# First modulation group taken straight as columns, and three products for one more feed-forward block, in a two-layer hybrid trunk on one core

## The chip, the core and the metric

The kernel runs on one core of a Trainium2 chip. A core has TensorE (PE: matrix products; its weight loads have a row of their own, PEld), VectorE (DVE), ScalarE (ACT), GpSimd (POOL) and SyncE (SP, which here only issues transfers). They work through queues of their own and wait for each other by semaphores. The metric is the device time of one execution in microseconds (us).

## The reference, cut to what matters

Two layers, each with a token mixer and a gated convolutional feed-forward. The mixer of layer 0 is a bidirectional mLSTM over 256 context and 256 latent tokens; that of layer 1 is latent attention, for which only the 256 latent tokens go on. Every sublayer's input is shifted and scaled by a modulation that is a product of a conditioning vector with a large matrix:

```python
def _modulation(cond, w, b):
    m = jax.nn.silu(cond) @ w + b
    return jnp.split(m[:, None, :], 6, axis=-1)
...
    hl = _modulate(x, ml[0], ml[1])         # x * (1 + scale) + shift
    hc = _modulate(xc, mc[0], mc[1])
...
def _conv_ffn(h, w_in, conv_w, conv_b, w_out):
    gate, up = jnp.split(h @ w_in, 2, axis=-1)
    return (jax.nn.silu(_dwconv(gate, conv_w, conv_b)) * up) @ w_out
```

There are two conditioning vectors (latent and context), the model width is 1024, and the matrix of one layer is 1024 x 6144. The first thing that the kernel needs is the shift and scale of layer 0's mixer, 2 x 1024 columns of that matrix.

## The kernel before, in words

**Precision.** Every fp32 operand is split into a high part (cast to fp32r by ACT, L388 or L323) and a low part (the difference, by DVE, L389 or L326). A product of two such operands is three matmuls, high-high, high-low, low-high (`mm3`, L383 to L385).

**Start.** `start_up` begins the mixer's up-projection while its inputs still arrive. The 1024 features are cut into four groups of 256 (`GROUPS`, 2 blocks of 128 each). `LOADS` lists the transfers in SP's order: `a` = the group's modulation weights (8 pieces into 4 tiles of 128 x 1024, L609), `r` = a weight tile of the up-projection, `x` = token tiles. `STEPS` lists by hand the order of work, and the order on PE, DVE and ACT is kept as written:

- `S g`: split the group's 4 modulation tiles (`ada_split`).
- `A g`: `ada_rows`, L474. The conditioning (128 x 4: two vectors, high and low) is the stationary operand, the weights stream through with 512 columns: 16 matmuls for 8 blocks of k and two parts, summed to a row block of 4 x 512. ACT copies it out of PSUM (L477).
- `T g`: `ada_T`, L484. Four transposes turn the rows into columns, 128 x 4 each.
- `M g`: `ada_cols` (L494, L495, DVE) adds the parts and the bias; `mod_tiles` scales and shifts the group's token tiles (L570, L572) and splits them into `hT`.
- `W m`: split up-projection weight tile m.
- `D n`: n products of a zero tile with itself into a PSUM tile that nobody reads ("idle", L659).
- two digits `m g`: the products of up tile m for group g.

The order of the steps of group 0 was S0, W0, A0, D3, T0, D6, M0.

**Last feed-forward.** `ffn_in` makes, for each of the 22 channel blocks p of 128, a gate tile (j = 0) and an up tile (j = 1) from 8 blocks of k. In layer 1 there are 256 tokens, and high and low parts of the input lie side by side (`both`). For p = 0 a tile takes three products of 256 columns a step of k. For p > 0 it takes two (L1320): the weights' high part with both parts of the input at once (512 columns, into the two halves of the PSUM tile), and the weights' low part with the high part (256 columns). Then ACT copies the right half out (L1323) and DVE adds it to the left (L1324), and the convolution (L668 to L675) and the gating (L1330) read that sum.

Of the kernel before, what the change touches and what calls it, by code (L numbers as in the profile page):

```python
# [47 lines left out]
GROUPS = ((0, 2), (2, 4), (4, 6), (6, 8))  # L48
LOADS = [(c[0], int(c[1])) for c in "a0 r0 r1 x0 r2 a1 r3 r4 x1 a2 x2 x3 a3".split()]
STEPS = [(c[0], int(c[1])) for c in (  # L50
    "S0 W0 A0 D3 T0 D6 M0 W1 W2 S1 00 01 W3 W4 A1 03 T1 M1 02 04 10 11 S2 A2 12 T2 M2 13 14 21 "
    "S3 20 A3 24 T3 22 23 M3 31 32 33 34 30").split()]

TAIL = {"mout": 4, "aout": 7, "fout1": 6}
# [300 lines left out]
class K:  # L355
# [97 lines left out]

    def ada_split(self, g):
        r = []
        for w in self.adaw.pop(g):
            hi, lo = [self.pool.tile([128, 1024], F32R, tag="u", name="adas", bufs=NU) for _ in range(2)]
            self.split(hi, lo, w)
            r.append((hi, lo))
        return r  # L460

    def ada_rows(self, g, parts):

        nc = self.nc
        f0, f1 = GROUPS[g]
        nf = f1 - f0
        n = 256 * nf
        pr = self.ps("adar")
        for i, (hi, lo) in enumerate(parts):
            for kk in range(1024 // n):  # L470
                k = i * (1024 // n) + kk
                c = slice(kk * n, (kk + 1) * n)
                for x in (hi, lo):
                    nc.tensor.matmul(pr[0:4, :n], self.condr[:, k, :], x[:, c], start=k == 0 and x is hi,  # L474
                                     stop=k == 7 and x is lo)
        r = self.s2("adarow")
        nc.scalar.copy(r[0:4, :n], pr[0:4, :n])  # L477
        return r
# [105 lines left out]
    def start_up(self):  # L584

        nc, st = self.nc, self.st
        self.hT = []
        self.xcd = self.dr.tile([16, 128, 512], F32, name="xcd")
        self.xmd = self.dr.tile([16, 128, 512], F32, name="xmd")
        self.t2d = {(n, p, j): self.dr.tile([128, 1024], F32, name="t2d")  # L590
                    for n, a, b in (("v", 2, 4), ("y", 1, 6)) for p in range(a) for j in range(b)}
        self.xA, self.x1, self.xc, self.xcr = {}, {}, [], []
        w, ps, raws = [], [], []
        src = self.a["ada_w"][0]
        self.adaw, self.xT = {}, []
        for op, g in LOADS:
            f0, f1 = GROUPS[g] if op != "r" else (0, 0)
            if op == "a":
                wd = 128 * (f1 - f0)
                nk = 512 // wd  # L600
                self.adaw[g] = []
                for k in range(8):
                    if k % nk == 0:
                        t = self.uf("adaw")
                        self.adaw[g].append(t)
                    ap = bass.AP(tensor=src.tensor, offset=src.offset + k * 128 * 6 * D + f0 * 128,
                                 ap=[[6 * D, 128], [D, 2], [1, wd]])
                    c = k % nk * 2 * wd
                    nc.sync.dma_start(t[:, c:c + 2 * wd].rearrange("p (a b) -> p a b", a=2), ap)  # L609
            elif op == "x":  # L610
                for i in range(f0, f1):
                    x = self.s2("xT")
                    nc.sync.dma_start(x, self.a["tokT"][i])
                    self.xT.append(x)
            else:
                n, _ = st.ids["up", g, 0]
                r = self.pool.tile([128, 1024], F32, tag="raw" if g < 3 else "ar", name="raw0",
                                   bufs=NRAW if g < 3 else 2)
                nc.sync.dma_start(r, st.ws[n])
                raws.append(r)  # L620

        def wsplit(m):
            if m < 3:
                t = self.pool.tile([128, 2, CW], F32R, tag="w", name="w", bufs=NB)
                h, l = t[:, 0], t[:, 1]
            elif m == 3:
                h, l = [self.pool.tile([128, CW], F32R, tag="acc", name="w0", bufs=2) for _ in range(2)]
            else:
                h, l = [self.pool.tile([128, CW], F32R, tag="u", name="w0", bufs=NU) for _ in range(2)]
            self.split(h, l, raws[m])  # L630
            w.append((h, l))
            ps.append(self.ps("up"))

        def part(g, ms):
            for m in ms:
                for k in range(*GROUPS[g]):
                    c = slice(k * 128, (k + 1) * 128)
                    self.mm3(ps[m], (w[m][0][:, c], w[m][1][:, c]), (self.hT[k][:, 0], self.hT[k][:, 1]),
                             k == 0, k == 7)

        e = mybir.EngineType
        idle = self.ps("idle")
        rows = {}
        with self.tc.manual_schedule(engines={e.PE, e.DVE, e.Activation}):
            for op, g in STEPS:
                if op == "S":
                    rows[g] = self.ada_split(g)
                elif op == "A":
                    rows[g] = self.ada_rows(g, rows[g])
                elif op == "T":  # L650
                    rows[g] = self.ada_T(g, rows[g])
                elif op == "M":
                    self.ada_cols(g, rows.pop(g))
                    self.mod_tiles(range(*GROUPS[g]))
                elif op == "W":
                    wsplit(g)
                elif op == "D":
                    for _ in range(g):
                        nc.tensor.matmul(idle, self.zero[:, 0:128], self.zero, start=True, stop=True)  # L659
                else:  # L660
                    part(int(op), [g])
        for m in range(NUP):
            self.up_evac(m, ps[m])
# [628 lines left out]
    def ffn_in(self, l, hT, n, nt, pre=(), both=None):  # L1292

        nc, st = self.nc, self.st
        cw, cb = self.smc("fcw%d" % l), self.smc("fcb%d" % l)
        key = "fin%d" % l
        acts = []
        pre = list(pre)
        for p in range(NF):
            pss = []  # L1300
            for j in range(2):
                if pre:
                    w, ps = pre.pop(0)
                    self.ffn_half(ps, w, hT, 1)
                    if not pre:
                        st.unhold()
                else:
                    w = st.use((key, p, j))
                    ps = self.ps("fin")
                    two = ps.rearrange("p (a t) -> p a t", a=2)  # L1310
                    for k in range(8):
                        c = slice(k * 128, (k + 1) * 128)
                        hi, lo = hT(k)
                        if both is None or p == 0:
                            self.mm3(ps[:, :n], (w[0][:, c], w[1][:, c]), (hi, lo), k == 0, k == 7)
                            continue

                        mms = [(two, w[0][:, c], both(k)), (ps[:, :n], w[1][:, c], hi)]
                        for i, (o, a, b) in enumerate(mms if k < 7 else mms[::-1]):
                            nc.tensor.matmul(o, a, b, start=k == 0 and i == 0, stop=k == 7 and i == 1)  # L1320
                    if both is not None and p > 0:
                        t = self.s2("fs")
                        nc.scalar.copy(t[:, n:2 * n], ps[:, n:2 * n])  # L1323
                        nc.vector.tensor_tensor(t[:, :n], ps[:, :n], t[:, n:2 * n], op=ALU.add)  # L1324
                        ps = t
                pss.append(ps)
                self.tick(nt, ADA_F if p else 0)
            tmp = self.s2("fg")
            self.conv(pss[0], [cw[:, j * NF + p:j * NF + p + 1] for j in range(3)], cb[:, p:p + 1], tmp, n)
            nc.vector.tensor_tensor(tmp[:, :n], tmp[:, :n], pss[1][:, :n], op=ALU.mult)  # L1330
            if l == 0:
                if p % 2:
                    self.act_sums(p // 2, acts.pop(), tmp)
                else:
                    acts.append(tmp)
                continue
            a = self.u("act")
            nc.scalar.copy(a[:, 0, :n], tmp[:, :n])
            nc.vector.tensor_sub(a[:, 1, :n], tmp[:, :n], a[:, 0, :n])
            acts.append(a)  # L1340
        return acts
# [642 lines left out]
```

## Time and profile before

| | |
|---|---|
| median of 3 runs | 1386.9 us (1386.04 to 1388.71) |
| the profiled execution | 1386.22 us |
| its span, first to last instruction | 1384.1 us |
| PE busy | 1354.0 us, 98% of the span |
| DVE busy | 1090.0 us, 79% |
| ACT busy | 713.1 us, 52% |
| mean granted clock of PE | 0.996 |

A row of the timeline reads: start in us, length in us, engine, line of the kernel, operation, output<-input, shapes, count, and in brackets the idle time before it and what ended it. "x4" rows are merged: the length goes from the first's start to the last's end. Matmuls are pipelined, so one's record is longer than the distance between two. A row of the groups reads: line, engine, operation, shapes, count, then busy us and mean ns of one, then idle time before them. A row of the stretches reads: from:to, length, then the busy time of PE, PEld, DVE, ACT and POOL, the granted clock of PE, the share of the DMA engines, GB/s.

### The profile page before, as it was taken

How to read it: one execution, taken by the hardware profiler on the slowest of the kernel's cores; microseconds unless marked ns; L12 is line 12 of the kernel's file. 1: busy time of each engine (PE TensorE's matmuls, PEld its weight loads, DVE VectorE, ACT ScalarE, POOL GpSimd, SP SyncE). 2: the span in 40 equal slices, each digit the busy share in tenths (PEclk: the TensorE clock that was granted, in tenths of full speed). 3: DMA queues.
4: the chain of work that ended last, by engine and by line, in shares of the span. 5: the costliest groups of instructions: out<-in, count | busy, mean ns of one | idle time of the engine just before them, and what ended most of it. 6: DMA issues, size and time to landing. Idle time of an engine off the chain costs nothing.

```text
span 1384.1 us, 18592 instructions
## 1 busy us (share of the span) xinstructions
PE 1354.0 (98%) x6567; PEld 1123.2 (81%) x6567; DVE 1090.0 (79%) x1768; ACT 713.1 (52%) x1221; POOL 121.6 (9%) x215
## 2 busy tenths in 40 slices
PE   7999999999999999999999999999999999999997
PEld 3788888888788888878898888888777888888886
DVE  6598857687688697779799878668898789788873
ACT  6585534435444555364643434334637567466660
POOL 0033000011011011120002000000001001000100
PEclk9999999999999999999999999999999999999999
DMA  9689847789666364766747877646987425256750
GB/s 338 227 293 316 290 156 247 239 286 302 214 200 204 105 232 132 250 193 228 241 147 239 300 230 234 212 145 229 312 231 226 137 99 202 109 185 185 252 202 31
DMA packets 97900, 297.58 MB, mean 215 GB/s; under 512 B 12136, under 2 KB 24808, under 8 KB 97808
## 3 DMA queue, kind: packets, MB, share of 16 engines
q1 hardware_dynamic: 68672, 218.52, 47.5%
q0 software_dynamic: 17472, 57.57, 13.3%
q10 hardware_dynamic: 11664, 20.32, 4.1%
q8 instruction: 51, 0.84, 0.2%
q14 instruction: 41, 0.34, 0.1%
HBM read 262.90 MB, written 33.46 MB: 214 GB/s over the span
## 4 chain that ended last, share of the span: by engine, by line
PE 91%; DVE 5%; ACT 2%; issue 1%; DMA 0%; SPq 0%; DVEq 0%; ACTq 0%
PE fin L1320 9%; PE fin L383 6%; PE fin L384 6%; PE fin L385 6%; PE tok L383 6%; PE tok L384 6%; PE tok L385 6%; PE y L384 5%; PE y L385 5%; PE y L383 5%; PE qk L383 4%; PE qk L385 4%; PE qk L384 4%; PE up L383 2%; PE up L385 2%; PE up L384 2%
## 5 line engine op out<-in xcount | busy, mean ns | idle before, releaser
L326 DVE TENSOR_TENSOR w<-raw,w 128x1024 fp32r<-128x1024 f32 (+3 forms) x290 | 348.1, 1203 | 141.3 <-ACT w L323 140.3
L323 ACT CAST w<-raw 128x1024 fp32r<-128x1024 f32 (+3 forms) x290 | 300.4, 1037 | 306.2 <-PE tok L385 88.6
L512 DVE SCALAR_TENSOR_TENSOR junk<-ar,bc 128x1024 f32<-128x1024 f32 x128 | 156.0, 1218 | 4.9 <-ACT bc L554 2.1
L384 PE MATMUL fin<-h,w 128*128 128x512 f32 (+1 forms) x376 | 141.2, 376 | 0.0
L385 PE MATMUL fin<-h,w 128*128 128x512 f32 (+1 forms) x376 | 140.9, 375 | 0.0
L383 PE MATMUL fin<-h,w 128*128 128x512 f32 (+1 forms) x376 | 140.8, 376 | 0.1
L1320 PE MATMUL fin<-h,w 128*128 128x256 f32 (+1 forms) x640 | 113.0, 339 | 0.0
L1320 PEld LDWEIGHTS fin<-h,w 128*128 128x128 f32 x640 | 98.2, 189 | 14.7
L383 PE MATMUL qk<-xc,w 128*128 128x512 f32 x256 | 100.7, 393 | 0.0
L385 PE MATMUL qk<-xc,w 128*128 128x512 f32 x256 | 99.9, 390 | 0.0
L384 PE MATMUL qk<-xc,w 128*128 128x512 f32 x256 | 99.8, 390 | 0.0
L384 PEld LDWEIGHTS fin<-h,w 128*128 128x128 f32 x376 | 70.8, 188 | 12.9 <-DVE h L1212 0.2
L385 PEld LDWEIGHTS fin<-h,w 128*128 128x128 f32 x376 | 70.8, 188 | 12.9
L383 PEld LDWEIGHTS fin<-h,w 128*128 128x128 f32 x376 | 70.5, 188 | 13.1 <-ACT h L1211 0.3
L383 PEld LDWEIGHTS qk<-xc,w 128*128 128x128 f32 x256 | 48.1, 188 | 10.0 <-issue 0.4
L385 PEld LDWEIGHTS qk<-xc,w 128*128 128x128 f32 x256 | 48.1, 188 | 9.9
L384 PEld LDWEIGHTS qk<-xc,w 128*128 128x128 f32 x256 | 48.1, 188 | 9.7
L383 PE MATMUL up<-hT,w 128*128 128x512 f32 x128 | 50.5, 394 | 0.5 <-ACT hT L388 0.5
L384 PE MATMUL up<-hT,w 128*128 128x512 f32 x128 | 50.1, 392 | 0.5 <-DVE hT L389 0.5
L385 PE MATMUL up<-hT,w 128*128 128x512 f32 x128 | 50.1, 391 | 0.3 <-DVE w L389 0.3
L383 PE MATMUL tok<-w,hT 128*128 128x512 f32 x128 | 49.8, 389 | 0.0
L384 PE MATMUL tok<-w,hT 128*128 128x512 f32 x128 | 49.8, 389 | 0.0
(463 smaller groups left out, 3151.2 us busy)
## 6 DMA issues: line engine op xcount, KB each, us to landing
raw<-in_ws SPq DMA_DIRECT2D x287, 512.0 KB, 4.3
ar<-in_adaT SPq DMA_DIRECT2D x80, 512.0 KB, 4.6
adaw<-in_ada_w SPq DMA_DIRECT2D x32, 256.0 KB, 6.7
t2d<-raw ACTq DMA_DIRECT2D x13, 512.0 KB, 4.9
raw<-t2d SPq DMA_DIRECT2D x13, 512.0 KB, 6.3
raw<-in_ws POOLq DMA_DIRECT2D x13, 512.0 KB, 8.0
zr<-fd ACTq DMA_DIRECT2D x33, 128.0 KB, 3.9
xmd<-xr POOLq DMA_DIRECT2D x16, 256.0 KB, 5.0
```

What stands on the lines that cost most here:

```text
L323: k.nc.scalar.copy(h[:, :cols], src)
L326: k.nc.vector.tensor_sub(l[:, :cols], src, h[:, :cols])
L383: mm(out, w[0], x[0], start=start, stop=False)
L384: mm(out, w[0], x[1], start=False, stop=False)
L385: mm(out, w[1], x[0], start=False, stop=stop)
L512: nc.vector.scalar_tensor_tensor(o, w, 1.0, self.bc[j], op0=ALU.mult, op1=ALU.mult, accum_out=col[:, k, j:j + 1])
L1320: nc.tensor.matmul(o, a, b, start=k == 0 and i == 0, stop=k == 7 and i == 1)
```

## The change

Group 0's modulation gets a step of its own, `C`, in place of `A` and `T`. `ada_direct` makes the weights the stationary operand, 128 columns at a time, and the conditioning the moving one, 4 columns wide: the result comes as columns, in the layout that the transposes gave. For each of 8 blocks of k, for the high and the low part, and for 4 column blocks there is one matmul, 64 in all, into one PSUM tile. After each of the first three weight tiles two idle products follow. The last weight tile of group 0 is split in two halves of 512 columns. The order becomes S0, D2, C0, W0, D5, M0. In `ffn_in` the three-product form is used for p < 2 instead of p = 0.

```diff
 STEPS = [(c[0], int(c[1])) for c in (
-    "S0 W0 A0 D3 T0 D6 M0 W1 W2 S1 00 01 W3 W4 A1 03 T1 M1 02 04 10 11 S2 A2 12 T2 M2 13 14 21 "
+    "S0 D2 C0 W0 D5 M0 W1 W2 S1 00 01 W3 W4 A1 03 T1 M1 02 04 10 11 S2 A2 12 T2 M2 13 14 21 "
     "S3 20 A3 24 T3 22 23 M3 31 32 33 34 30").split()]
...
     def ada_split(self, g):
         r = []
-        for w in self.adaw.pop(g):
+        ws = self.adaw.pop(g)
+        for w in ws:
             hi, lo = [self.pool.tile([128, 1024], F32R, tag="u", name="adas", bufs=NU) for _ in range(2)]
-            self.split(hi, lo, w)
+            n = 512 if g == 0 and w is ws[-1] else 1024
+            for i in range(0, 1024, n):
+                self.split(hi[:, i:i + n], lo[:, i:i + n], w[:, i:i + n])
             r.append((hi, lo))
         return r
+
+    def ada_direct(self, g, parts, idle):
+
+        f0, f1 = GROUPS[g]
+        n = 2 * (f1 - f0)
+        pt = self.ps("adat")
+        for i, (hi, lo) in enumerate(parts):
+            for kk in range(8 // n):
+                k = i * (8 // n) + kk
+                for x in (hi, lo):
+                    for j in range(n):
+                        c = (kk * n + j) * 128
+                        self.nc.tensor.matmul(pt[:, 4 * j:4 * j + 4], x[:, c:c + 128], self.condr[:, k, :],
+                                              start=k == j == 0 and x is hi, stop=k == 7 and j == n - 1 and x is lo)
+            for _ in range(2 if i + 1 < len(parts) else 0):
+                self.nc.tensor.matmul(idle, self.zero[:, 0:128], self.zero, start=True, stop=True)
+        return pt
...
+                elif op == "C":
+                    rows[g] = self.ada_direct(g, rows[g], idle)
...
-                        if both is None or p == 0:
+                        if both is None or p < 2:
                             self.mm3(ps[:, :n], (w[0][:, c], w[1][:, c]), (hi, lo), k == 0, k == 7)
                             continue
...
-                    if both is not None and p > 0:
+                    if both is not None and p > 1:
                         t = self.s2("fs")
                         nc.scalar.copy(t[:, n:2 * n], ps[:, n:2 * n])
```

## The prediction

> **What bounds the kernel now.** I read the page's first, second and fourth parts, to see which engine sets the end.
>
> ```profile
> span 1384.1 us, 18592 instructions
> PE 1354.0 (98%) x6567; PEld 1123.2 (81%) x6567; DVE 1090.0 (79%) x1768; ACT 713.1 (52%) x1221; POOL 121.6 (9%) x215
> PE 91%; DVE 5%; ACT 2%; issue 1%; DMA 0%; SPq 0%; DVEq 0%; ACTq 0%
> ```
>
> TensorE (PE) is busy 98% of the span and owns 91% of the chain that ended last. So an edit is worth something in two places only: where PE's own work gets longer or shorter, and where PE stands idle. The busy time by stretches (PE is the first column after the length) says where it stands idle.
>
> ```profile
> 26.80:590.00 563.20, 563.17 (x2541) 459.06 (x2539) 426.72 (x675) 280.32 (x480) 64.92 (x114) 1.00 0.70 232
> 590.00:1185.00 595.00, 585.04 (x2910) 493.47 (x2908) 498.46 (x826) 305.92 (x534) 45.71 (x81) 1.00 0.65 213
> 1196.00:1376.00 180.00, 180.00 (x1009) 156.49 (x1008) 134.83 (x212) 102.74 (x170) 9.82 (x16) 1.00 0.51 168
> ```
>
> From 26.8 on PE hardly stops; what happens before 26.8 shifts everything behind it one for one. The first edit lies in those 27 us, the second at 1196, where PE has no gap at all. The chain in order of time shows the start:
>
> ```profile
> 4.72 5.90 DMA adaw<-in_ada_w
> ...
> 10.64 1.06 ACT adas L388
> ...
> 11.73 1.24 DVE adas L389
> ...
> 13.01 0.86 PE adar L474 x3
> 13.87 0.69 PE idle L659 x3
> 14.56 0.40 PE adat L484 x4
> ...
> 14.98 0.18 DVE adt L494
> ```
>
> The chain runs through the last weight tile's load, its cast, its subtraction, the last row products, the copy of the row (hidden here behind "idle"), the transposes, and the add. All of the start hangs on the moment at which VectorE (DVE) begins L494: 14.98. Behind L494 on DVE and behind L572, which waits for it, on ScalarE (ACT) stand, in order, the first token tiles and the splits W1, W2, S1, W3, W4:
>
> ```profile
> 19.37 2.36 DVE L389 TENSOR_TENSOR w<-raw,w 128x1024 fp32r<-128x1024 f32 x2 [0.26 <-ACT w L388]
> 21.65 4.62 DVE L389 TENSOR_TENSOR adas<-adaw,adas 128x1024 fp32r<-128x1024 f32 x4
> 26.19 2.35 DVE L389 TENSOR_TENSOR w<-raw,w 128x1024 fp32r<-128x1024 f32 x2
> ```
>
> DVE works there without a gap for 9 us and none of these rows waits for a DMA, so a later L494 is not caught up. **The first edit's worth is the new start of L494 minus 14.98.**
>
> **The change part by part.** Before, group 0 takes 16 products with 4 weight columns and 512 moving columns, a copy and four transposes. After, it takes 64 products (8 k, high and low half, 4 column blocks), each loading 128 weight columns for 4 moving ones. When the operands come does not change, for the casts hang on the DMA and the subtractions on the casts:
>
> ```profile
> 0.95 0.48 DVE L436 MEMSET zero<- 128x512 f32 x1
> ...
> 6.79 0.59 PE L474 MATMUL adar<-adas,condr 128*4 128x512 f32 x1 [6.79 <-ACT adas L388]
> 8.05 1.87 PE L474 MATMUL adar<-adas,condr 128*4 128x512 f32 x4 [0.67 <-DVE adas L389]
> 10.12 2.56 PE L474 MATMUL adar<-adas,condr 128*4 128x512 f32 x8 [0.20 <-DVE adas L389]
> 11.73 1.23 DVE L389 TENSOR_TENSOR adas<-adaw,adas 128x1024 fp32r<-128x1024 f32 x1 [0.19 <-ACT adas L388]
> 13.01 0.86 PE L474 MATMUL adar<-adas,condr 128*4 128x512 f32 x3 [0.33 <-DVE adas L389]
> 16.69 0.50 PE L383 MATMUL up<-hT,w 128*128 128x512 f32 x1 [0.16 <-ACT hT L388]
> ```
>
> The high half of tile 0 is there at 6.79, its low half at 8.05; those of tiles 1 and 3 at 10.12 and 12.96 (11.73 + 1.23), and that of tile 2 between. The rows also give the clock. At 8.05 four products need 1.87: (1.87 - 0.59)/3 = 0.43 a product. At 13.01 three need 0.86: (0.86 - 0.39)/2 = 0.23, with 0.39 for a single one at full speed (L384 below). So PE runs at half speed at first; the eight products from 10.12 on take 2.56, which is two slow distances and five fast ones with the 0.39 and a short wait, so the clock rises at about 10.95.
>
> *Price of one weight load and product.* The trace has no 128-column fp32r load before a 4-column product, so I bound it. Durations of loads (mean ns is the last number before the second bar):
>
> ```profile
> L474 PEld LDWEIGHTS adar<-adas,condr 128*4 128x4 f32 x64 | 5.0, 87 | 20.8 <-ACT adas L388 7.1 <-DVE adas L389 6.8 <-issue 1.1
> L857 PEld LDWEIGHTS gates<-xc,w 128*32 128x32 f32 x32 | 3.5, 109 | 3.8
> L383 PEld LDWEIGHTS qk<-xc,w 128*128 128x128 f32 x256 | 48.1, 188 | 10.0 <-issue 0.4
> L1754 PEld LDWEIGHTS PT<-ident,P 128*128 128x128 f32 x64 | 7.2, 140 | 0.1
> 14.53 0.32 PEld L484 LDWEIGHTS adat<-ident,adarow 4*128 4x128 f32 x4 [0.40 <-ACT adarow L477]
> 14.53 0.41 PE L484 MATMUL adat<-ident,adarow 4*128 4x4 f32 x4
> L384 PE MATMUL qk<-xc,w 128*128 128x512 f32 x256 | 99.8, 390 | 0.0
> L484 PE MATMUL adat<-ident,adarow 4*128 4x4 f32 x4 | 0.4, 203 | 0.0
> 1190.85 0.41 PE L383 MATMUL fin<-h,wu 128*128 128x256 f32 x1
> 1191.06 0.41 PE L384 MATMUL fin<-h,wu 128*128 128x256 f32 x1
> 1194.04 0.28 PE L385 MATMUL fin<-h,wu 128*128 128x256 f32 x1
> ...
> 1196.56 0.28 PE L385 MATMUL fin<-h,wu 128*128 128x256 f32 x1
> ```
>
> A product's fp32r load lasts 87 ns at 4 columns, 109 at 32 and 188 at 128: (188 - 109)/96 = 0.82 ns a column, so 128 columns hold the load path about 105 ns. Upper row: 256-column products with 128-column loads start every (1196.56 - 1194.04)/21 = 0.12; load and stream both fit in that. Lower row: the transposes, also 128 columns loaded for 4 moving ones, pass at (0.41 - 0.20)/3 = 0.07 (by their loads 0.06); but their kind of load lasts 140 at 128 columns (L1754), not 188. **I take 0.12**, as the new loads are of the 188 kind, and keep 0.06 as the other end. At half speed the 256-column products start every 1191.06 - 1190.85 = 0.21, so 0.21 there, and 0.12 for the cheap end.
>
> *The sum of the first edit.* From 8.05, twelve pairs of tile 0 at 0.213: 2.56, to 10.61. Two idle products across the rise, 0.43 + 0.23, to 11.27. Tile 1: 16 x 0.12 = 1.92, to 13.19; two idle 0.46, to 13.65; tile 2 to 15.57; idle to 16.03; tile 3 to 17.95. No tile waits for its low half any more: PE itself is the bound. The last product starts 0.12 before that, ends 0.20 later (18.03), and L494 starts at 18.06 instead of 14.98: **+3.1 us**. The copy and the transposes that go are in this difference already.
>
> The other pieces lie under this. D2 can run from about 1.5 us, once the zero tile is written (L436), and PE has nothing until 6.79; without that cover it would cost 0.86. D5 (5 x 0.23 = 1.15) ends before the first "up" product, which needs both adds, a modulation and a cast after L494: 16.69 - 14.98 = 1.7; D6 was hidden in the same way. Halving the last tile gives ACT and DVE one more instruction each and lets DVE start earlier; PE reaches tile 3 only at 16.03, so it neither gains nor costs; were PE faster, the halves would save about four pairs. W0's cast and subtraction come before M0 on both engines as before, and are done long before 18. SP's queue is untouched, POOL has nothing here.
>
> The added wait is L494's on PE, 3 us longer. Queued behind it are M0 and the five splits above; PE's "up" products wait for those, with nothing else to do.
>
> Bounds: at the full clock from 8.05 on, the same sum ends L494's wait at 16.75 (+1.8). The rise comes at the end of a stretch whose phase nothing here fixes; each us that it comes later adds about 0.44. At 0.107 a pair instead of 0.12, the 48 fast pairs save 0.6.
>
> *The second edit.* For the second channel block of the last feed-forward, 16 steps of k (2 tiles of 8) go from two products (512 and 256 columns) to three of 256.
>
> ```profile
> 1196.68 5.78 PE L1320 MATMUL fin<-h,wu 128*128 128x512 f32 x32
> 1202.30 9.90 PE L1320 MATMUL fin<-h,w 128*128 128x512 f32 x55
> ```
>
> The two-product form takes (1202.30 - 1196.68)/16 = 0.351 a step, the three-product form 3 x 0.12 = 0.36: 16 x 0.009 = **+0.14 us** on PE, without cover. It saves two copies on ACT and two adds on DVE, but PE has no gap from 1196 to 1376, so these are worth nothing, and their absence cannot bring the term below 0.
>
> Together: 3.1 + 0.14 = +3.2 us on the profiled 1386.22 (span 1384.1 and 2.1 around it), 1389.4. That execution lies 0.7 below the median of 1386.9; I state the forecast against the median: **1390.1**.
>
> **The rivals.**
>
> *A: the clock stays at half speed through group 0.* The clock is seen to fall and rise at 1079.5: it fell after a stretch that PE filled by half (row 1), and then took 3.1 us at half speed, with PE working all the time, before it rose.
>
> ```profile
> 1076.30:1079.50 3.20, 1.60 (x10) 1.01 (x9) 3.20 (x7) 2.79 (x9) 0.00 (x0) 1.00 0.00 0
> 1079.50:1082.60 3.10, 3.10 (x12) 3.10 (x13) 3.10 (x9) 1.97 (x6) 0.00 (x0) 0.50 0.00 0
> 7.75:10.95 3.20, 2.70 (x7) 0.57 (x8) 2.11 (x3) 2.40 (x3) 0.00 (x0) 1.00 1.04 382
> ```
>
> Before, PE streams wide products for 2.70 of the 3.2 us ahead of the rise. After, mostly weights are loaded there; the two idle products of a tile stream 0.86 in a round of 4.3. If only streaming counts, that is 20%, less than the half-filled stretch after which the clock fell. Then 10.61, + 0.86, + 3.41 (16 x 0.213), and so on: tile 3 ends at 23.4, L494 starts at 23.5: +8.5 + 0.14, 1395.5. For it: the small streams. Against it: the weight loads fill the time, and no row says that they do not count. The Trainium skill, "TensorE: Matmul & The Clock Gate", Part 1, says that the gate goes by how busy PE was in windows of 3413 ns and is at half rate by default; the 3.1 us stretch agrees roughly, and by that rule, read strictly, this case would follow. Chance 0.15.
>
> *B: the rise comes one stretch later*, at about 14.1. Then tile 1 runs 12.6 pairs slow and 3.4 fast (to 14.56), tile 2 ends at 16.94, tile 3 at 19.32; L494 at 19.43: +4.45 + 0.14, 1391.5. For and against as in A, with loads counting in part. Chance 0.14.
>
> *C, the other side: a pair costs 0.06*, as the transposes' loads do. Then tile 0 ends at 9.49, the idle products at 10.35, tile 1 at 11.61, tile 2 at 13.03, tile 3 at 14.45, L494 at 14.62: -0.36 + 0.14, 1386.7, not slower. It decides where a fast pair costs less than 0.071: 72 q + 8.05 + 0.66 + 0.92 + 0.23 = 14.98. Its floor is the data: low half of tile 3 at 12.96, four pairs, L494 at 13.4, -1.5 + 0.14, 1385.5. For it: the transposes load as many columns. Against it: 188 against 140 ns, and the even 0.82 a column. The Trainium skill, "TensorEngine Tiling (Array Packing)", Instruction Overhead, gives a matmul about 60 cycles however small its free size, and names no weight load beside it; by that rule this case would follow, and no row here shows such a pair in fp32r. Chance 0.19.
>
> *D: the delay is won back later*, where PE waits for others between 590 and 1185 (10 us of 595). The chain there runs through DVE and ACT work that shifts too. Chance 0.04, about 1387.
>
> **How the numbers follow.** Forecast 0.48, A 0.15, B 0.14, C 0.19, D 0.04. The range goes from C's floor, 1385.6, to 1393.6: B plus a late phase, plus what the runs shown spread upward. It leaves out A and some tails. A measurement of this kernel can tell about 0.2%, 2.8 us, from no change. The forecast's +3.2 lies just beyond it, with bounds +1.8 to +4: slower in 0.7 of its cases. With A and B: 0.34 + 0.15 + 0.14, and a little, 0.66 slower. Same: 0.14 of the forecast, most of C, D: 0.29. Faster: 0.05, for no case reaches it but by the runs' spread.
>
> **What would show it.** L494's first start near 18.1 (14.6 in C, 19.4 in B, 23.5 in A); starts of the new products 0.12 apart, 0.21 at first; the first "up" product about 1.7 after L494; PE then the same until 1196, and p = 1 of the last feed-forward 0.36 a step. Wrong would be my price of a pair, or the clock's rise.

## The result and the profile after

| | before | after |
|---|---|---|
| median of 4 runs each | 1386.47 us (1385.11 to 1388.71) | 1393.91 us (1393.57 to 1395.20) |
| profiled execution | 1386.22 us | 1393.86 us |
| its span | 1384.1 us | 1391.8 us |

The ratio is 1.0054 (95%: 1.0036 to 1.0071): slower by 7.4 us, where +3.2 had been forecast. The sign was right; the time lies 0.3 us beyond the upper end of the range.

The first, second and fourth parts of the page of the kernel after:

```profile
span 1391.8 us, 18714 instructions
PE 1363.8 (98%) x6631; PEld 1137.6 (82%) x6631; DVE 1088.7 (78%) x1767; ACT 712.8 (51%) x1219; POOL 121.3 (9%) x215
PE 87%; DVE 6%; DMA 3%; issue 1%; ACT 1%; SPq 0%; DVEq 0%; ACTq 0%
```

PE's share is the same 98%, of a longer span. The page cannot show the cause: a PE at half speed counts as busy, and so does one that mostly loads weights. The timeline of the start of the kernel after can (start, length, engine, line, operation; L476 are the new products, L479 and L681 idle products, L514 is the add that was L494; the row at 16.54 stands twice, once cut off after eight pairs):

```profile
7.43 1.01 PE L476 MATMUL adat<-condr,adas 128*128 128x4 f32 x4 [4.71 <-ACT adas L388]
8.69 2.72 PE L476 MATMUL adat<-condr,adas 128*128 128x4 f32 x12 [0.25 <-DVE adas L389]
11.27 1.20 PE L479 MATMUL idle<-zero 128*128 128x512 f32 x2
12.27 3.41 PE L476 MATMUL adat<-condr,adas 128*128 128x4 f32 x16
16.54 1.70 PE L476 MATMUL adat<-condr,adas 128*128 128x4 f32 x8
16.54 3.41 PE L476 MATMUL adat<-condr,adas 128*128 128x4 f32 x16
20.80 3.41 PE L476 MATMUL adat<-condr,adas 128*128 128x4 f32 x16
24.07 2.48 PE L681 MATMUL idle<-zero 128*128 128x512 f32 x5
24.25 0.17 DVE L514 TENSOR_TENSOR adt<-adat,sm 128x8 f32<-128x8 f32 x1 [9.20 <-PE adat L476]
26.35 0.63 PE L383 MATMUL up<-hT,w 128*128 128x512 f32 x1
28.43 0.50 PE L384 MATMUL up<-hT,w 128*128 128x512 f32 x1
30.91 4.62 DVE L389 TENSOR_TENSOR adas<-adaw,adas 128x1024 fp32r<-128x1024 f32 x4
```

Read the lengths of the merged rows. A pair is a load and its product. At 16.54 eight pairs last 1.70 and sixteen last 3.41: (3.41 - 1.70)/8 = 0.214 a pair, the half-speed price. The rows of the second and fourth tile have the same length, and the first tile's twelve pairs, with 0.35 for the last product's own length, give (2.72 - 0.35)/11 = 0.215. The five idle products at 24.07 take 2.48: (2.48 - 0.59)/4 = 0.47 each, where 0.23 is full speed. So the clock did not rise during group 0. The first "up" product, at 26.35, still lasts 0.63; the one at 28.43, 0.50, is the first short one. DVE waits 9.20 us for PE at L514, which starts at 24.25 instead of 14.98: **+9.27 us**. Of these, 0.64 come from data: tile 0's low half is used at 8.69 instead of 8.05 in this execution. The rest, 8.6, is the pairs and the idle products between them, all at half speed, in place of the rows. The kernel before was also early in its profiled execution: in the profiles of runs 1 and 4 below, which leave group 0 as it was, that add starts at 14.93 and at 15.85. So up to 0.9 of the 9.27 belongs to the execution and not to the change.

The delay is passed on whole: group 1's four subtractions start at 30.91 instead of 21.65, +9.26. The tile views of "dkv" in layer 1 (duration min/median/max in ns, then first and last start) carry it further. Before:

```profile
L383 PE MATMUL dkv<-w,hc x16: 308/309/416, 1046.8 to 1053.5; 128*128 128x320 f32 x16
L383 PE MATMUL dkv<-w,hl x16: 306/309/472, 1078.4 to 1087.0; 128*128 128x320 f32 x16
```

After:

```profile
L383 PE MATMUL dkv<-w,hc x16: 309/309/417, 1056.1 to 1062.8; 128*128 128x320 f32 x16
L383 PE MATMUL dkv<-w,hl x16: 307/309/415, 1087.8 to 1094.8; 128*128 128x320 f32 x16
```

It is still +9.3 at the first row and +9.4 at the start of the second. The second row then ends at 1094.8 instead of 1087.0, only +7.8: before, the sixteen products lasted 8.6 us, now 7.0, because the half-speed stretch that the prediction quoted at 1079.5 is not there in this execution. A second half-speed stretch, at the last normalisation, is there in both. In the profiled executions of the eight kernels below such late stretches come and go (two had both, four only the first, one only the second, one neither), so this 1.6 is taken as no merit of the change.

The last feed-forward's two-product form, in the timeline of the kernel after:

```profile
1209.84 0.28 PE L385 MATMUL fin<-h,wu 128*128 128x256 f32 x1
1209.96 14.24 PE L1342 MATMUL fin<-h,w 128*128 128x512 f32 x80
```

Block p = 2 begins at 1209.96 instead of 1202.30, +7.66, and the span grew by 7.7. The account of these two executions closes to 0.1: 9.3 at the start, 1.6 less at "dkv", 0.14 more for the second edit: 7.8.

### The profile page after: what moved, and what is told of

The parts are those of the page before. It is cut to its first block, busy times and chain, and to the rows that moved or that the text cites. A ratio compares the mean times of both kernels' runs of the same rounds, so it can differ in the third digit from the quotient of the medians.

```text
span 1391.8 us, 18714 instructions
## 1 busy us (share of the span) xinstructions
PE 1363.8 (98%) x6631; PEld 1137.6 (82%) x6631; DVE 1088.7 (78%) x1767; ACT 712.8 (51%) x1219; POOL 121.3 (9%) x215
## 4 chain that ended last, share of the span: by engine, by line
PE 87%; DVE 6%; DMA 3%; issue 1%; ACT 1%; SPq 0%; DVEq 0%; ACTq 0%
PE fin L1342 8%; PE fin L383 6%; PE fin L384 6%; PE fin L385 6%; PE tok L383 6%; PE tok L384 6%; PE tok L385 6%; PE y L384 5%; PE y L385 4%; PE y L383 4%; PE qk L383 4%; PE qk L385 4%; PE qk L384 4%; PE up L383 2%; PE up L385 2%; PE up L384 2%
```

## The experiments

**The theories.** S: only wide products, which stream for most of their time, move the clock; weight loads with 4-column products do not, so the change took away what had raised it. L: loads count as work like any other. P: the clock is not the matter, a 128-column load with its product simply takes 0.21. The second edit was the other suspect.

**1. second_edit_alone.** The kernel before with only the second edit:

```diff
-                        if both is None or p == 0:
+                        if both is None or p < 2:
...
-                    if both is not None and p > 0:
+                    if both is not None and p > 1:
```

> The kernel before with the second edit alone (three products also for p = 1). All theories of the first edit are silent here. By the prediction: the sixteen steps of k of p = 1 take 0.36 us each instead of 0.351, +0.14 us, so no difference that can be measured (ratio 1.000, within 0.001). A rival: the loss of 7.4 us lies partly here, because the convolution and the gating now hold two PSUM tiles longer; then the time is 1 us or more above the kernel before, and PE shows a gap between p = 0 and p = 4 of the last feed-forward.

Measured: 1385.79 us (11 runs) against 1386.99 (15 runs), ratio 0.9994 (0.9985 to 1.0003). Its timeline at p = 1:

```profile
1196.43 0.28 PE L384 MATMUL fin<-h,wu 128*128 128x256 f32 x1
...
1201.95 20.23 PE L1320 MATMUL fin<-h,w 128*128 128x512 f32 x114
```

There are 46 distances from 1196.43 to 1201.95: 5.52/46 = 0.12, so 0.36 a step, as the term had it. The gap of the rival is not there: PE is busy for 179.92 of the 180 us from 1196 on. The edit makes no difference that can be measured; +0.14 is far below that.

**2. first_edit_alone.** The kernel after without the second edit:

```diff
-                        if both is None or p < 2:
+                        if both is None or p == 0:
...
-                    if both is not None and p > 1:
+                    if both is not None and p > 0:
```

> The changed kernel without the second edit. If the first edit carries the loss: between +6.5 and +8 us on the kernel before, with the first L494-type add (first modulation add on DVE) at about 24 us again and the column products 0.21 apart. If the second edit carried part of it, that part is missing here.

Measured: 1394.94 us (4 runs) against 1386.99, ratio 1.0060 (1.0046 to 1.0074). Its start:

```profile
20.53 3.41 PE L476 MATMUL adat<-condr,adas 128*128 128x4 f32 x16
23.98 0.17 DVE L514 TENSOR_TENSOR adt<-adat,sm 128x8 f32<-128x8 f32 x1 [9.67 <-PE adat L476]
```

The last tile's row has the length of half speed again, 3.41, and the first add comes 9.0 late. The whole loss lies in the first edit.

**3. no_idle_between.** The kernel after without the idle products between the tiles. By S they raise nothing and only cost time.

```diff
-            for _ in range(2 if i + 1 < len(parts) else 0):
+            for _ in range(0):
```

> The changed kernel without the six idle products between the four weight tiles. Theory S (only streamed columns raise the clock; 64 column products at half speed whatever the idle ones do): the six idle products are dead weight of 0.43 each, so the first add comes 2.6 us earlier, at about 21.7, and the kernel takes about 5 us more than the one before instead of 7.4. Theory L (weight loads do count, the clock stayed down for another reason, a gap or the phase): the clock can rise within the column products, with or without idle ones; the first add then lies anywhere between 16 and 21.7. Theory P (a column product costs 0.21 at any clock): the same 21.7, so this run tells S and P from L, not from each other.

Measured: 1392.33 us (4 runs), ratio 1.0042 (1.0028 to 1.0055).

```profile
8.77 12.96 PE L476 MATMUL adat<-condr,adas 128*128 128x4 f32 x60 [0.25 <-DVE adas L389]
21.59 2.48 PE L681 MATMUL idle<-zero 128*128 128x512 f32 x5
21.77 0.17 DVE L514 TENSOR_TENSOR adt<-adat,sm 128x8 f32<-128x8 f32 x1 [7.37 <-PE adat L476]
```

With 0.35 for the last one's own length, the sixty pairs are (12.96 - 0.35)/59 = 0.214 apart, and the add starts 2.48 earlier than after: the six idle products bought nothing. No rise of the clock shows within them, which speaks against L; the run does not part S from P.

**4. columns_for_group_2.** The kernel before, with the new step (`ada_direct` as in the change, without its idle products) for group 2 instead of group 0, at a place where the clock is up and wide products stand on both sides:

```diff
-    "S0 W0 A0 D3 T0 D6 M0 W1 W2 S1 00 01 W3 W4 A1 03 T1 M1 02 04 10 11 S2 A2 12 T2 M2 13 14 21 "
+    "S0 W0 A0 D3 T0 D6 M0 W1 W2 S1 00 01 W3 W4 A1 03 T1 M1 02 04 10 11 S2 C2 12 M2 13 14 21 "
...
+                elif op == "C":
+                    rows[g] = self.ada_direct(g, rows[g], idle)
```

> The kernel before, with the column form (no idle products) for group 2 in place of its row products and transposes; there PE runs at the full clock and without a gap. Removed on PE: 16 row products of 0.23 and four transposes, 4.0 us. Theory P (0.21 a pair at any clock): all 64 pairs 0.21 apart from the first, 13.6 us, and the products behind them 0.23 apart as before: +9.6 us. Theory S (streamed columns alone count): the pairs start 0.12 apart, after 3 to 6.5 us the clock falls and the rest are 0.21 apart, and the wide products behind run 0.43 apart for some 3 us: +5 to +9 us. Theory L (loads count): 64 pairs 0.12 apart throughout, 7.7 us, +3.7 us, no fall of the clock.

Measured: 1393.95 us (4 runs), ratio 1.0054 (1.0038 to 1.0069). Its timeline, with the 64 pairs merged up to three different ends:

```profile
35.39 2.06 PE L473 MATMUL adat<-condr,adas 128*128 128x4 f32 x18
35.39 4.08 PE L473 MATMUL adat<-condr,adas 128*128 128x4 f32 x36
35.39 8.77 PE L473 MATMUL adat<-condr,adas 128*128 128x4 f32 x64
44.02 0.77 PE L383 MATMUL up<-hT,w 128*128 128x512 f32 x1
47.58 0.40 PE L385 MATMUL up<-hT,w 128*128 128x512 f32 x1
47.81 0.39 PE L383 MATMUL up<-hT,w 128*128 128x512 f32 x1
```

From the 18th to the 36th pair: (4.08 - 2.06)/18 = **0.112 a pair** at the full clock. That refutes P, and shows the forecast's 0.12 to be a little high. But 64 pairs at 0.112 would take 7.2, not 8.77. The busy times of its stretches (after the length: PE, PEld, DVE, ACT, POOL, then the granted clock) show why:

```profile
39.40:40.40 1.00, 1.00 (x11) 1.00 (x10) 0.00 (x0) 0.00 (x0) 0.00 (x0) 1.00 1.09 389
40.40:41.40 1.00, 1.00 (x8) 1.00 (x8) 0.00 (x0) 0.00 (x0) 0.00 (x0) 0.67 1.01 400
41.40:42.40 1.00, 1.00 (x6) 1.00 (x6) 0.00 (x0) 0.00 (x0) 0.00 (x0) 0.50 1.02 410
44.40:47.40 3.00, 3.00 (x8) 2.32 (x8) 2.06 (x5) 2.80 (x5) 0.00 (x0) 0.50 0.93 373
```

PE and the load path are both busy for 1.00 of every us, with no gap, and yet the granted clock falls at about 40.7 (0.67 is full speed for a third of that us and half speed for the rest). It returns at about 47.5, when the products are 0.23 apart again, 3.5 us after the wide ones resumed at 44.02. That refutes L, and is the direct sight of S. The loss in the profiled execution is 8.6 us of pairs in place of 3.7 of row products (sixteen at 0.23) and 0.4 of transposes, and 3.5 us of "up" products at half speed: 4.5 + 1.8 = 6.3, and the span grew by 6.0.

**5. warm_before_columns.** If the clock is up before the pairs start, how long does it hold? The kernel after with twelve idle products ahead instead of two:

```diff
-STEPS = [(c[0], int(c[1])) for c in (
+STEPS = [(c[0], int(c[1:])) for c in (
-    "S0 D2 C0 W0 D5 M0 W1 W2 S1 00 01 W3 W4 A1 03 T1 M1 02 04 10 11 S2 A2 12 T2 M2 13 14 21 "
+    "S0 D12 C0 W0 D5 M0 W1 W2 S1 00 01 W3 W4 A1 03 T1 M1 02 04 10 11 S2 A2 12 T2 M2 13 14 21 "
```

> The changed kernel with twelve idle products ahead of the column products in place of two (from 1.5 us, 0.43 each, to 6.7). Theory S (streamed columns alone move the clock): the clock rises before or soon after the first pairs, so these start 0.11 apart; with the two idle products a tile the wide streaming is then 20% of the time, the clock falls again 3 to 6.5 us later, and the rest is 0.21 apart: the first add at 18 to 22 us instead of 24.2. Theory G (the gaps between 2.7 and 8.7 kept the clock down, weight loads would have held it up): it stays up throughout and the first add comes at about 17.0. Both agree that even then the first add is later than the 14.98 of the kernel before, since 60 pairs of 0.11 and six idle products do not fit between 8.05 and 15.

Measured: one execution, 1394.79 us beside 1386.21 of the kernel before. Timeline:

```profile
1.50 4.45 PE L681 MATMUL idle<-zero 128*128 128x512 f32 x12 [1.50 <-DVE adav L447]
7.61 0.68 PE L476 MATMUL adat<-condr,adas 128*128 128x4 f32 x4 [1.66 <-ACT adas L388]
24.43 0.17 DVE L514 TENSOR_TENSOR adt<-adat,sm 128x8 f32<-128x8 f32 x1 [9.98 <-PE adat L476]
```

And its stretches:

```profile
7.00:9.00 2.00, 0.81 (x5) 0.73 (x5) 1.23 (x1) 1.58 (x2) 0.00 (x0) 0.75 1.05 327
13.00:15.00 2.00, 2.00 (x11) 2.00 (x10) 1.23 (x1) 0.19 (x1) 0.00 (x0) 0.50 1.05 407
27.00:29.00 2.00, 2.00 (x6) 0.99 (x6) 1.01 (x3) 1.78 (x3) 0.00 (x0) 0.63 1.10 349
```

The twelve products raise the clock: at half speed throughout they would take 11 x 0.43 + 0.59 = 5.3, not 4.45. Then PE stands for 1.66 us until the first weights come, and the clock falls at 8.0 (0.75 over 7 to 9), four pairs into group 0; in the 3.4 us before that, from 4.6 on, PE was busy for 1.74. It stays at 0.50 until about 28.5. Both numbers expected for the first add were missed, for neither saw the fall come so early. That the clock holds once it is up, as theory G has it, is refuted, and that pairs and thin idle products do not raise it is confirmed again, over the 15 us from 9 to 24.

**6. eight_idle_between.** The kernel after with eight idle products after a tile instead of two, so that wide products fill about half of the time at full speed:

```diff
-            for _ in range(2 if i + 1 < len(parts) else 0):
+            for _ in range(8 if i + 1 < len(parts) else 0):
```

> The changed kernel with eight idle products after each of the first three weight tiles in place of two. Theory S: eight of 0.43 fill a stretch of 3.4 us with streaming, so the clock rises during or after the first eight, at 14 to 18 us, and the pairs behind are 0.11 apart; at that clock half of the time is streamed and the clock holds or just falls. The first add comes at 24 to 27 us, as late as now, though 18 products of 0.43 were added (7.7 us at half speed). Theory P (0.21 a pair at any clock) is gone already; if the clock does not rise here, S is wrong too, and the first add comes at 32 us.

Measured: one execution, 1395.65 us.

```profile
11.17 3.76 PE L479 MATMUL idle<-zero 128*128 128x512 f32 x8
14.73 2.11 PE L476 MATMUL adat<-condr,adas 128*128 128x4 f32 x16
16.70 2.10 PE L479 MATMUL idle<-zero 128*128 128x512 f32 x8
18.64 1.84 PE L476 MATMUL adat<-condr,adas 128*128 128x4 f32 x16
20.34 2.09 PE L479 MATMUL idle<-zero 128*128 128x512 f32 x8
24.15 0.17 DVE L514 TENSOR_TENSOR adt<-adat,sm 128x8 f32<-128x8 f32 x1 [9.83 <-PE adat L476]
```

And its stretches:

```profile
15.30:25.50 10.20, 10.07 (x67) 8.82 (x66) 0.75 (x3) 0.92 (x2) 0.00 (x0) 1.00 1.07 369
25.50:28.90 3.40, 2.30 (x6) 1.15 (x7) 2.07 (x4) 2.77 (x5) 0.00 (x0) 1.00 1.09 348
28.90:32.30 3.40, 3.40 (x9) 1.73 (x8) 3.40 (x4) 3.40 (x5) 0.00 (x0) 0.51 1.09 363
```

Eight idle products at half speed raise the clock, and the pairs behind them, the same instructions as after, go from 3.41 a tile to 1.84; cut off after nine pairs the row lasts 1.06, so (1.84 - 1.06)/7 = 0.11 each. With eight of 0.23, 1.84, in a round of 3.64 (16.70 to 20.34), about half, the clock holds. It falls once more at 28.9, for 3.4 us, behind a stretch in which PE waited for its token tiles and was busy for 2.30 of 3.40. What is won by speed is spent on the idle products: the add stands at 24.15, as after.

**7. halves_alone.** The kernel before with the last modulation tile split in two halves:

```diff
-            self.split(hi, lo, w)
+            n = 512 if g == 0 and w is ws[-1] else 1024
+            for i in range(0, 1024, n):
+                self.split(hi[:, i:i + n], lo[:, i:i + n], w[:, i:i + n])
```

> The kernel before with only the last weight tile of group 0 split in halves, with row products and transposes as before. The last row product then waits for a half: one product of 0.23 is left behind the last subtraction instead of three, so the first add comes 0.4 to 0.5 us sooner after the end of the last subtraction (2.0 us before). The time changes by less than a measurement can tell.

Measured: one execution, 1387.25 us beside 1386.21.

```profile
9.46 5.38 PE L477 MATMUL adar<-adas,condr 128*4 128x512 f32 x15 [0.67 <-DVE adas L389]
11.12 2.43 DVE L389 TENSOR_TENSOR adas<-adaw,adas 128x1024 fp32r<-128x1024 f32 x3 [0.25 <-ACT adas L388]
15.96 0.17 DVE L497 TENSOR_TENSOR adt<-adat,sm 128x8 f32<-128x8 f32 x1 [0.91 <-PE adat L487]
```

The last subtraction ended at 13.55 and the add came 2.41 later, not the 1.5 expected: in this execution the weights were late (9.46, not 8.05), PE waited, and the fifteen row products were mostly at half speed themselves: 5.38 against 14 x 0.23 + 0.39 = 3.6. What the halves are worth by themselves is not shown by it.

**8. warm_before_rows.** The rows of before with the clock raised ahead of them, the one version to which the theory points: rows stream, so they should keep it.

```diff
-STEPS = [(c[0], int(c[1])) for c in (
+STEPS = [(c[0], int(c[1:])) for c in (
-    "S0 W0 A0 D3 T0 D6 M0 W1 W2 S1 00 01 W3 W4 A1 03 T1 M1 02 04 10 11 S2 A2 12 T2 M2 13 14 21 "
+    "S0 W0 D18 A0 D3 T0 D6 M0 W1 W2 S1 00 01 W3 W4 A1 03 T1 M1 02 04 10 11 S2 A2 12 T2 M2 13 14 21 "
```

> The kernel before with eighteen idle products ahead of the row products of group 0, from 1.5 us on, so that the clock is up when the first weights come and no long gap lets it fall. The row products stream 512 columns each, so by theory S the clock then holds: all row products 0.23 apart, and the first add 2.0 us after the last subtraction, as in the profiled execution of before, where the clock rose in time anyway. Where it rises late (as in the run with halves alone, where the add came 2.4 us after) this saves 0.4 us or more. In the median 0 to 0.7 us less than before, not more than a measurement can tell. If the idle products run on past 9 us because the clock rises late, they delay the rows and the time is up by as much as 1 us.

Measured: 1386.97 us (11 runs) against 1386.33 (15 runs), ratio 1.0004 (0.9995 to 1.0013). The profiled execution was the slowest of the eleven, 1391.62, so its trace is read for the start alone:

```profile
1.49 6.59 PE L659 MATMUL idle<-zero 128*128 128x512 f32 x18 [1.49 <-DVE adav L447]
8.70 1.10 PE L474 MATMUL adar<-adas,condr 128*4 128x512 f32 x4 [0.38 <-DVE adas L389]
15.74 0.17 DVE L494 TENSOR_TENSOR adt<-adat,sm 128x8 f32<-128x8 f32 x1 [0.73 <-PE adat L484]
```

The row products do run at full speed from the first tile on, (1.10 - 0.39)/3 = 0.24 a product, but then they wait for the next subtraction, which is DVE's and not PE's to hasten (and the first came at 8.70 here, not 8.05): nothing is won. The last subtraction ends at 13.73 there, and the add comes 2.0 later, as expected. No version here measurably beats the kernel before.

## Why the prediction was wrong

**What bounds the kernel** was right: the first edit's worth was the new start of the first add minus 14.98, and that shift was found again at group 1 (+9.26) and at "dkv" (+9.3).

**When the operands come** was right but for the 0.64 us of this execution. No tile waited for its low half after tile 0; PE itself was the bound, as said.

**The price of a pair** was right: 0.214 at half speed (0.213 taken), 0.112 at full (0.12 taken, about 0.105 the estimate from load durations). The cheap end of 0.06, and with it rival C, is excluded by the 0.112 in run 4. The Trainium skill, "TensorEngine Tiling (Array Packing)", Instruction Overhead, names about 60 cycles for a matmul however narrow and no weight load beside it; the prediction let rival C follow from that, and the 0.112 us measured with a load for every product stands against it: the measurement decides.

**The step that failed** is the line "Two idle products across the rise, 0.43 + 0.23, to 11.27", and with it every 0.12 after it. It carried the rise of the clock at 10.95 over from the kernel before, where wide row products raised it, to a kernel in which loads had taken their place. The clock rose at about 28.4. At half speed the 48 pairs behind that line cost 48 x (0.213 - 0.12) = 4.5 more and the six idle products 1.0 more, and this 5.5 is the whole distance, within 0.1, from the forecast's 18.06, plus 0.64 for the later data, to the measured 24.25. The sign came out right, and for the reason given, that PE itself is the bound; the size did not. Rival A, put at 0.15 and left out of the range, is what happened: it had this add at 23.5, which with the later data is 24.1, and 24.25 was measured. Its change of +8.6 is still 1.2 above the measured +7.4. The profiled executions show two things that can shift a time by that much, the moment at which the first weights come and the half-speed stretches late in the kernel; how much of the 1.2 is either is not shown. The evidence named against A, that the loads fill the time, was the wrong measure: in run 4 they filled all of it and the clock fell.

On the time scale the Trainium skill, "TensorE: Matmul & The Clock Gate", Part 1, gives windows of 3413 ns that run freely; the fall at 40.7 and the return at 47.5 in run 4 are two of these apart, and wide products raised the clock after 3.5 us. That agrees. Part 1 speaks of how busy PE was, and the prediction read that as busy in the profile's sense; 1.00 busy beside a falling clock (run 4) says that it cannot be read so. The same page, Why this matters for your kernels, asks for no idle gaps above about 3 us between bursts; in run 5 a pause of 1.66 us with pairs behind it was enough. The measurement decides.

**The second edit**, +0.14, was right in size by the distances (0.36 a step) and too small to be seen in the time.

**Rivals B and D.** B did not happen: no rise came one stretch later, at 14.1, as the 0.214 of tiles 2 and 3 show. Nor did D: the 1.6 us at "dkv" is a half-speed stretch that one execution had and the other did not, not slack that took up the delay, which was still whole where that stretch begins.

**What stays open.** The granted clock reads 1.00 at the start, in the kernel after for instance over the pairs that are 0.214 apart, up to the first change that the trace records; so half speed there is read from distances alone. How much streaming it takes is not settled either. Two idle products in a round of 4.27 us, 20%, did not raise the clock, and eight in a round of 3.64, half, held it. But the prediction's row that ends at 1079.5 (PE busy for 1.60 of 3.20) and the 1.74 of 3.40 in run 5 were both followed by a fall. The worth of the halves alone is not shown.

## What to carry to other kernels

When a product is turned round so that the big operand becomes the stationary one, price it twice: by the time of a load and its product, and by what the change does to the clock of everything around it. Count how long PE streams wide products, not how long it is busy, in each stretch of some 3.5 us (the time in which wide products brought the clock back in run 4) before and after; if the change takes the streaming away, take every price there at half speed. Idle products that streamed for about half of the time held the clock here (run 6), those that streamed for a fifth did not raise it, and the half cost what it won.

## What the runs showed of the hardware

- The granted clock fell 5.3 us after the first pair (35.39 to 40.7), though the loads and PE were busy to the last; it returned 3.5 us after wide products resumed (run 4).
- A load of 128 fp32r columns with a 4-column product goes at one per 0.112 us at the full clock and one per 0.214 at half. The load slows with the clock too: its record lasts 192 ns (the median in run 4) and 333 ns (in the kernel after).
- About 20% of streaming, beside pairs, did not raise the clock in the 12.8 us from 11.27 to 24.07 (after); about half held it from 15.3 until the last pairs at 24 (run 6).
- A clock that twelve wide products had raised fell at 8.0, after a pause of 1.66 us and four pairs (run 5).
- What raises the clock need be neither many stationary columns nor other values than zero: the row products of the kernel before have four such columns (0.43 apart at 8.05, 0.23 at 13.01), and the idle products of run 5 are of a zero tile (twelve in 4.45 us, not 5.3).
